# Gate and up projections by Strassen's method with seven quarter products, feed-forward groups four blocks wide

## The chip, the cores and the metric

The kernel runs on one NeuronCore of a Trainium2 chip. The metric is the device time of one execution in microseconds (us). The engines are named as the profile names them: PE (TensorE, with its weight loads as PEld), DVE (VectorE), ACT (ScalarE), POOL (GpSimd) and SP (the queue that issues most transfers). SBUF is the on-chip memory that the engines work from; PSUM is the small memory of eight banks into which PE writes its products.

## The reference

Two layers of an encoder, for 640 tokens (512 of a prompt and 8 x 16 of samples), model width 1024. Each layer has three mixing branches, an output projection, a feed-forward part and a gated projection of a second input. The change touches the feed-forward part alone:

```
x = x + merged @ prm['w_out']
hf = rms_norm(x, prm['norm_ffn'])
g, up = jnp.split(hf @ prm['w_ffn_in'], 2, axis=-1)
x = x + (jax.nn.silu(g) * up) @ prm['w_ffn_out']
ple_gate = jax.nn.sigmoid(rms_norm(x, prm['norm_ple']) @ prm['w_ple_gate'])
```

`w_ffn_in` is 1024 x 5632: 2816 columns of the gate and 2816 of up. `w_ffn_out` is 2816 x 1024. All is float32.

## The kernel before

**Layout.** Activations lie transposed: 128 partitions of features by 640 tokens, eight such slices for the model width. A projection gives 128 output features for two halves of 320 tokens, each half in its own PSUM bank, and runs over eight slices of the contraction (k = 0 to 7).

**Float32 by three products.** Each operand is split into a high part, rounded to PE's fast float format (ACT, a copy), and a low part, the rest (DVE, one subtraction). A product is the sum of three matmuls: high x high, high x low, low x high. So one projection of 128 features takes 8 x 2 x 3 = 48 matmuls of 320 columns (`rows`; the matmuls are recorded at L274).

**Weights.** They come in chunks of 128 x 1024 numbers (512 KB), in the order of a table of units that is made before the kernel (`layer_units`). `load_chunk` issues the transfer into `raw` (two buffers) and records the split into `hi` (ACT, L220) and `lo` (DVE, L221), with a priority ahead of the other work; `hi` and `lo` have three buffers each. `next_chunk` keeps three chunks loaded ahead.

**Feed-forward part.** The 2816 hidden features are 22 blocks of 128, in groups of 8, 8 and 6. For each block (`u_ffn`) the gate chunk and the up chunk give 48 matmuls each. DVE scales the products by the norm of the token (`scaled`, L338) out of PSUM, ACT takes the silu of the gate (L756), POOL multiplies (L760), ACT and DVE split the result into the group's `mid` tiles (L277, L278). After the last block of a group the eight slices of the down projection run over the group's blocks (`u_ffo`): 8 x 2 x 3 = 48 matmuls a slice for a group of 8, and DVE adds them to `x` (L741).

**The norm.** `norm` scales each slice of `x` by the gain (ACT, L307), makes its low part (DVE, L308), squares it (ACT, L309) and sums the squares (DVE, L311). PE adds over the partitions (tile `cs`), POOL takes the power (L317), and PE spreads the result over the partitions (tiles `sp`). The scale of a token is applied to the products, not to the operands, so PE starts on slice k as soon as that slice is split.

**Order.** The program is recorded in the order of the units. A scheduler then sets each engine's order by priority and by its own estimates, and gives each tile a buffer; every engine works through its list in that order, and an instruction that waits holds up all behind it on its engine. Products lie in four PSUM banks (tile `pd`); a bank is free again when DVE (or ACT) has read it.

Of the kernel before, what the change touches and what calls it, by code (L numbers as in the profile page):

```python
# [9 lines left out]
F32 = mybir.dt.float32  # L10
# [11 lines left out]
NT = NP + NS  # L22
# [45 lines left out]
def layer_units():  # L68
    units = []

    def full(name, arg, w, cols):
        units.append((name, arg, [_chunk(w, range(KD), cols)]))

    def av(j):
        c = _cols("av", 256 * j, 256)
        units.append(("av", j, [_chunk("w_in", range(0, 4), c), _chunk("w_in", range(4, 8), c)]))

    def branch(b, c):
        ch = [_chunk("w_in", range(KD), _cols("g" + b, 128 * c, 128))]
# [41 lines left out]
CHUNKS = [ch for u in UNITS for ch in u[2]]  # L121
NCH = len(CHUNKS)
CHW = [sum(len(c) for _, _, c in ch) for ch in CHUNKS]

C_ID, C_CM, C_ADM, C_CMS, C_T, C_BO, C_IND, C_PAR, C_N = 0, 128, 256, 384, 400, 416, 418, 426, 442
G_MIX, G_FFN, G_PLE, G_BIAS, G_Q, G_K, G_N = 0, 8, 16, 24, 48, 49, 50
# [41 lines left out]
        self.kind, self.gen, self.due, self.held, self.past = kind, gen, due, False, False  # L168


class Net:
    def __init__(self, tc, A, cst, big, wp, wk, sm, ps):
        nc = tc.nc
# [30 lines left out]
    def load_chunk(self, pieces=1, also=None):  # L204
        nc, i = self.nc, self.n_loaded
        self.n_loaded += 1
        w = CHW[i % NCH] // pieces
        raw = self.wp.tile([128, 1024], F32, tag="raw", name=f"raw{i}", bufs=2)
        hi = self.wp.tile([128, 1024], F32R, tag="hi", name=f"hi{i}")
        lo = self.wp.tile([128, 1024], F32R, tag="lo", name=f"lo{i}")  # L210
        low = nc.gpsimd if LO_POOL[0] <= i % NCH < LO_POOL[1] else nc.vector
        for p in range(pieces):
            c = slice(w * p, w * p + w)
            nc.sync.dma_start(raw[:, c], self.A["w"][i // NCH, i % NCH, :, c])
            if also:
                also(p)

            def split(c=c):
                with self.tc.high_priority(offset=200):
                    nc.scalar.activation(hi[:, c], raw[:, c], AF.Copy)  # L220
                    low.tensor_tensor(lo[:, c], raw[:, c], hi[:, c].bitcast(F32), op=OP.subtract)  # L221
# [66 lines left out]
    def qk2(self, name):  # L288
        return self.ps.tile([128, 2, 512], F32, tag="qk", name=name, bufs=NQ)

    def pair(self, pool, tags):
        return [pool.tile([128, KD, NT], F32R, tag=t, name=t, bufs=1) for t in tags]

    def norm(self, x, g0, xh, xl):
        nc, gl = self.nc, self.gl
        acc = self.wk.tile([128, NT], F32, tag="t", name="nacc")
        for k in range(KD):
# [18 lines left out]
        nc.vector.tensor_scalar(rsc, cs[:, :5], 1.0 / D, EPS, op0=OP.mult, op1=OP.add)  # L316
        nc.gpsimd.tensor_tensor(rsc, rsc, self.half[:, :5], op=OP.pow)  # L317
# [28 lines left out]
    def layer(self, l):  # L346
# [1 line left out]
        self.S = S = {}  # L348
        self.sc, self.si = [], []
        self.busy = False  # L350
        self.mh = self.norm(self.x, G_MIX, *self.pair(self.big, ("xh", "xl")))
# [372 lines left out]
    def u_out(self, c, ch):  # L724
        S = self.S
        if c == 0:
            mh, ml = self.pair(self.big, ("xh", "xl"))
# [9 lines left out]
    def addx(self, c, pt):  # L737
        x = self.S["x"]
        for h in range(2):
            sl = slice(HN * h, HN * h + HN)  # L740
            self.nc.vector.tensor_tensor(x[:, c, sl], x[:, c, sl], pt[h][:, :HN], op=OP.add)  # L741

    def u_ffn(self, a, ch):
        nc, S = self.nc, self.S
        gi, m = a
        first = gi == 0 and m == 0
        if first:
            S["fx"] = self.norm(S["x"], G_FFN, *self.pair(self.at, ("fh", "fl")))
# [7 lines left out]
        nc.scalar.activation(g, g, AF.Silu)  # L756
# [3 lines left out]
        nc.gpsimd.tensor_tensor(u, u, g, op=OP.mult)  # L760
        self.split(S["mid"][0][:, m], S["mid"][1][:, m], u)

    def u_ffo(self, a, ch):
        gi, c = a
        self.addx(c, self.rows(ch[0], 0, FGROUPS[gi], *self.S["mid"], both=(c == 0)))

    def u_ple(self, c, ch):
        nc, S, l = self.nc, self.S, self.l
        if c == 0:
            S["fx"] = self.norm(S["x"], G_PLE, *self.pair(self.at, ("fh", "fl")))  # L770
            pb = self.at.tile([128, 2, 2, NT], F32R, tag="pb", name="pb", bufs=1)
            for k in range(2):
                pr = self.at.tile([128, NT], F32, tag="lb", name="pr")
# [446 lines left out]
```

## Time and profile before

| | |
|---|---|
| median of 3 runs | 2503.01 us (2500.07 to 2503.66) |
| the profiled execution | 2500.76 us, its span 2499.0 us |
| granted PE clock | 0.995 |
| PE busy, share of the span | 2443.1 us, 98% |
| DVE | 1357.0 us, 54% |
| ACT | 935.5 us, 37% |
| POOL | 317.6 us, 13% |
| feed-forward part, each layer | 466.84 us, of which DVE is busy 197.6 us and ACT 113.5 us |

The profile shows one execution. Busy time counts instructions in work; a matmul's own duration (about 309 ns) overlaps with the next, which starts 147 ns later. The feed-forward part runs from the end of the output projection to the first matmul of the gated projection behind it: from 711.61 to 1178.45 us in the first layer and from 1954.04 to 2420.88 us in the second.

### The profile page before, as it was taken

The numbers are of one execution on the slowest core, as the hardware profiler recorded it, in microseconds if no ns is written. First come the engines' busy times: TensorE is split into PE (matmuls) and PEld (weight loads), VectorE is DVE, ScalarE is ACT, GpSimd is POOL, SyncE is SP. The second block draws the span as 40 slices with busy tenths as digits, with TensorE's granted clock in tenths as the row PEclk, the third lists the DMA queues.
The fourth block names the chain that finished last, engine by engine and source line by source line (L and its number), as shares of the span: only waits on it lengthen the run. The fifth ranks groups of instructions, "written<-read, shape, count | busy, mean of one in ns | idle before, by whom it ended". The sixth has DMA issues, their size and how long they took to land. (4 is left out here: it accounts for less than half of the span.)

```text
span 2499.0 us, 42360 instructions
## 1 busy us (share of the span) xinstructions
PE 2443.1 (98%) x17528; PEld 2335.2 (93%) x17528; DVE 1357.0 (54%) x2447; ACT 935.5 (37%) x1361; POOL 317.6 (13%) x375
## 2 busy tenths in 40 slices
PE   8989999999999999999999999999999999999999
PEld 8887788899999999999999877888999999999999
DVE  5885865544544344345558858556446443443454
ACT  5654466522332122123345454655224221221231
POOL 1122421100001001010011323220000010110100
PEclk9999999999999999999999999999999999999999
DMA  6223244532322222222342232445323222222222
GB/s 200 86 74 88 70 142 138 182 102 74 125 75 76 77 71 74 76 72 81 100 144 87 68 92 87 128 147 166 101 76 129 77 75 77 69 77 76 70 84 75
DMA packets 102399, 242.89 MB, mean 97 GB/s; under 512 B 11152, under 2 KB 33952, under 8 KB 102208
## 3 DMA queue, kind: packets, MB, share of 16 engines
q1 hardware_dynamic: 99552, 229.81, 29.7%
q0 software_dynamic: 2656, 10.38, 1.2%
q8 instruction: 138, 2.26, 0.4%
q14 instruction: 53, 0.43, 0.1%
HBM read 221.07 MB, written 19.08 MB: 96 GB/s over the span
## 5 line engine op out<-in xcount | busy, mean ns | idle before, releaser
L220 ACT ACTIVATE hi<-raw 128x1024 fp32r<-128x1024 f32 (+4 forms) x306 | 316.4, 1035 | 1093.5 <-PE pd L274 654.7
L274 PE MATMUL pd<-fh,lo 128*128 128x320 f32 x1664 | 513.5, 309 | 0.0
L274 PE MATMUL pd<-fh,hi 128*128 128x320 f32 x1664 | 513.4, 309 | 0.0
L274 PE MATMUL pd<-fl,hi 128*128 128x320 f32 x1664 | 513.1, 308 | 0.0
L274 PE MATMUL pd<-xh,hi 128*128 128x320 f32 x1568 | 497.1, 318 | 0.0
L274 PE MATMUL pd<-xh,lo 128*128 128x320 f32 x1568 | 490.9, 313 | 2.4 <-DVE lo L221 2.4
L274 PE MATMUL pd<-xl,hi 128*128 128x320 f32 x1568 | 491.4, 314 | 0.0
L221 DVE TENSOR_TENSOR lo<-raw,hi 128x1024 fp32r<-128x1024 f32 (+4 forms) x268 | 366.7, 1369 | 141.0 <-ACT hi L220 139.9
L274 PEld LDWEIGHTS pd<-fh,hi 128*128 128x128 f32 x1664 | 312.4, 188 | 0.1
L274 PEld LDWEIGHTS pd<-fh,lo 128*128 128x128 f32 x1664 | 312.4, 188 | 0.0
L274 PEld LDWEIGHTS pd<-fl,hi 128*128 128x128 f32 x1664 | 312.4, 188 | 0.0
L274 PEld LDWEIGHTS pd<-xh,hi 128*128 128x128 f32 x1568 | 297.0, 190 | 15.2 <-issue 13.5
L274 PE MATMUL pd<-mid,hi 128*128 128x320 f32 x1408 | 309.9, 308 | 0.0
L274 PEld LDWEIGHTS pd<-xl,hi 128*128 128x128 f32 x1568 | 297.3, 190 | 7.3 <-issue 6.1
L274 PEld LDWEIGHTS pd<-xh,lo 128*128 128x128 f32 x1568 | 297.2, 190 | 7.0 <-DVE lo L221 2.9
L274 PEld LDWEIGHTS pd<-mid,hi 128*128 128x128 f32 x1408 | 235.4, 188 | 0.0
L274 PE MATMUL pd<-mid,lo 128*128 128x320 f32 x704 | 217.0, 308 | 0.0
L760 POOL TENSOR_TENSOR fu<-fu,fg 128x640 f32<-128x640 f32 x44 | 68.9, 1566 | 772.2 <-DVE fu L338 772.2
L741 DVE TENSOR_TENSOR x<-x,pd 128x320 f32<-128x320 f32 x128 | 61.6, 486 | 193.4 <-PE pd L274 192.0
L338 DVE TENSOR_TENSOR fu<-pd,rs 128x320 f32<-128x320 f32 x88 | 43.2, 491 | 192.0 <-PE pd L274 192.0
L274 PEld LDWEIGHTS pd<-mid,lo 128*128 128x128 f32 x704 | 132.2, 188 | 0.0
L338 DVE TENSOR_TENSOR gt<-pd,rs 128x320 f32<-128x320 f32 x96 | 47.0, 490 | 154.8 <-PE pd L274 154.5
(264 smaller groups left out, 3730.5 us busy)
## 6 DMA issues: line engine op xcount, KB each, us to landing
raw<-w SPq DMA_DIRECT2D x270, 512.0 KB, 3.6
kc<-c_k SPq DMA_DIRECT2D x64, 256.0 KB, 4.6
kc<-c_v SPq DMA_DIRECT2D x64, 256.0 KB, 3.5
raw<-w SPq DMA_DIRECT2D x16, 384.0 KB, 3.1
raw<-w SPq DMA_DIRECT2D x11, 468.0 KB, 3.8
ka<-b_k SPq DMA_DIRECT2D x16, 256.0 KB, 3.4
kv<-b_v SPq DMA_DIRECT2D x16, 256.0 KB, 3.3
x<-xT SPq DMA_DIRECT2D x8, 320.0 KB, 6.0
```

What stands on the lines that cost most here:

```text
L220: nc.scalar.activation(hi[:, c], raw[:, c], AF.Copy)
L221: low.tensor_tensor(lo[:, c], raw[:, c], hi[:, c].bitcast(F32), op=OP.subtract)
L274: self.nc.tensor.matmul(out, a, b, start=start, stop=stop)
L338: self.nc.vector.tensor_tensor(dst[:, sl], pt[h][:, :HN], self.rs[:, sl], op=OP.mult)
L741: self.nc.vector.tensor_tensor(x[:, c, sl], x[:, c, sl], pt[h][:, :HN], op=OP.add)
L760: nc.gpsimd.tensor_tensor(u, u, g, op=OP.mult)
```

## The change

**Seven products in place of eight.** For one block take the gate rows and the up rows of the weights, each in two halves of the contraction (k = 0 to 3 and 4 to 7): A11, A12 (gate) and A21, A22 (up); and the normed activations in the same halves and in two halves of the tokens: B11, B12 and B21, B22. The two outputs for two halves of tokens are eight products of such quarters before. Now they are seven: A11 B11, A12 B21, S1 T1, S2 T2, S3 T3, S4 B22 and A22 T4, with S1 = A21 + A22, S3 = A11 - A21, S2 = A22 - S3, S4 = A12 - S2, and T1 = B12 - B11, T3 = B22 - B12, T2 = B11 + T3, T4 = B21 - T2. Each has 4 slices x 3 matmuls = 12 matmuls of 320 columns, in one PSUM bank, so a block takes 84 matmuls where it took 96. The outputs are sums of the products: `u2` = A11 B11 + S2 T2, `u3` = `u2` + S3 T3, `u4` = `u2` + S1 T1; gate = (A11 B11 + A12 B21, `u4` + S4 B22), up = (`u3` + A22 T4, `u3` + S1 T1).

**The weights' sums** are made on the chip, for every block, from the two raw chunks (`load_second`): four sums of 128 x 512 on DVE, and five splits of 128 x 512 (ACT the high part, DVE the low), for S1, S3, S2, A22 and S4. The first chunk of a block is split as before. The second raw chunk has one buffer of its own (`rawb`), S2 to S4 have four (`sh`, `sl`).

**The activations' sums** are made once a layer (`norm_quarters`): for k = 0 to 3 the scaled slice, its split for B11, T1 and its split; for k = 4 to 7 T3, T2, T4 and B21, B22 with their splits. B11, T1, T2, T3 lie in `fh` and `fl`, and B21, B22, T4 in `xh` and `xl`, which the output projection reads up to its end.

**The products' sums** replace `scaled`: ACT copies A11 B11 out, DVE makes seven sums of 128 x 320 out of PSUM, then multiplies up and gate by the norm, 128 x 640 each. Silu, product and split follow as before.

**Groups and order.** The 22 blocks are in groups of 4, 4, 4, 4, 3 and 3, with two buffers for `mid`. The eight slices of a group's down projection are dealt out among the blocks of the next group, and one chunk holds two slices; those of the last group follow at the end. A slice of a group of four takes 24 matmuls. The sums into `x` (two a slice, on DVE) are now for 6 x 8 slices in place of 3 x 8. The second input's transfers (`pr`) and split (`pb`), which stood at the beginning of the output projection, use the buffers of `mid` and stand in the last group's down projection.

```diff
-FGROUPS = (8, 8, 6)
+FGROUPS = (4, 4, 4, 4, 3, 3)
...
+            if gi:
+                for c in range(KD * m // n, KD * (m + 1) // n):
+                    ffo(gi - 1, c)
+    for c in range(KD):
+        ffo(gi, c)
...
+    def load_second(self, i):
+
+        nc, r0 = self.nc, self.raw
+        r1 = self.at.tile([128, 1024], F32, tag="rawb", name=f"raw{i}", bufs=1)
+        nc.sync.dma_start(r1, self.A["w"][i // NCH, i % NCH])
...
+        def split(src, h, l):
+            nc.scalar.activation(h, src, AF.Copy)
+            nc.vector.tensor_tensor(l, src, h.bitcast(F32), op=OP.subtract)
...
+            nc.vector.tensor_tensor(s1, r1[:, a], r1[:, b], op=OP.add)
+            split(s1, hi[:, a], lo[:, a])
...
+            nc.vector.tensor_tensor(s3, r0[:, a], r1[:, a], op=OP.subtract)
+            own(s3)
...
+            nc.vector.tensor_tensor(s2, r1[:, b], s3, op=OP.subtract)
+            own(s2)
+            split(r1[:, b], hi[:, b], lo[:, b])
...
+            nc.vector.tensor_tensor(s4, r0[:, b], s2, op=OP.subtract)
+            own(s4)
...
+    def norm_quarters(self, x, g0):
...
+            nc.scalar.activation(q, xk, AF.Copy, scale=g)
...
+            nc.scalar.activation(sq, x[:, k], AF.Square)
+            if k < 4:
+                self.split(o1[0][:, 0, j], o1[1][:, 0, j], q[:, 0])
+                nc.vector.tensor_tensor(b[:, j, 0], q[:, 1], q[:, 0], op=OP.subtract)
+                self.split(o1[0][:, 1, j], o1[1][:, 1, j], b[:, j, 0])
+            else:
+                p = a[:, j]
+                nc.vector.tensor_tensor(p[:, 1], q[:, 1], p[:, 1], op=OP.subtract)
+                nc.vector.tensor_tensor(p[:, 0], p[:, 0], p[:, 1], op=OP.add)
+                self.split(o1[0][:, 2:4, j], o1[1][:, 2:4, j], p)
+                self.split(o2[0][:, 0:2, j], o2[1][:, 0:2, j], q)
+                nc.vector.tensor_tensor(q[:, 0], q[:, 0], p[:, 0], op=OP.subtract)
+                self.split(o2[0][:, 2, j], o2[1][:, 2, j], q[:, 0])
...
-        pg = self.rows(ch[0], 0, KD, *S["fx"], both=first)
...
-        self.scaled(pg, g)
...
+        p1 = prod("A11", "B11")
+        nc.scalar.activation(r1, p1, AF.Copy)
+        if first:
+            p5, p7 = prod("S1", "T1"), prod("S3", "T3")
+        p6 = prod("S2", "T2")
...
+        add(u2, p6, r1)
+        if not first:
+            p7 = prod("S3", "T3")
+        add(u3, p7, u2)
+        if not first:
+            p5 = prod("S1", "T1")
+        add(u[:, t], p5, u3)
+        add(u4, p5, u2)
+        add(g[:, h], prod("A12", "B21"), r1)
+        add(u[:, h], prod("A22", "T4"), u3)
+        nc.vector.tensor_tensor(u, u, rs, op=OP.mult)
+        add(g[:, t], prod("S4", "B22"), u4)
+        nc.vector.tensor_tensor(g, g, rs, op=OP.mult)
         nc.scalar.activation(g, g, AF.Silu)
```

In the built program PE has 15,880 matmuls and transposes where it had 16,408; DVE has 3,043 instructions where it had 2,319, ACT 1,523 where it had 1,263, POOL and SP as many as before. Up to the output projection of a layer every engine's order is what it was. Line numbers in the rows below are those of the changed kernel where they stand for it (L242 is the old L221, L335 the old L278, L806 the old L741; L262, L272 to L282 are the weights' sums and their low parts, L872 the products' sums, L897 and L899 the products with the norm).

**DVE, a block inside the second group.** Before, from the scaling of one block's gate on to the next (`fg` the gate, `fu` up, `lo` a chunk's low part, `mid1` the low part of the result):

```order
L338 TENSOR_TENSOR fg_8246<-pd_8196,rs_7504 128x320
L338 TENSOR_TENSOR fg_8246<-pd_8197,rs_7504 128x320
L221 TENSOR_TENSOR lo89_8192<-raw89_8190,hi89_8191 128x1024
L338 TENSOR_TENSOR fu_8300<-pd_8250,rs_7504 128x320
L338 TENSOR_TENSOR fu_8300<-pd_8251,rs_7504 128x320
L221 TENSOR_TENSOR lo90_8308<-raw90_8306,hi90_8307 128x1024
L278 TENSOR_TENSOR mid1_7453<-fu_8300,mid0_7452 128x640
```

After, the part of a block between its S2 T2 and the multiplication of up by the norm (`xh2` holds r1, u2, u3, u4, `xl2` the gate, `sl` the low parts of S2 to S4):

```order
L872 TENSOR_TENSOR xh2_7552<-pd_8727,xh2_7552 128x320
L262 TENSOR_TENSOR sl_8835<-s2_8832,sh_8834 128x512
L872 TENSOR_TENSOR xh2_7552<-pd_8741,xh2_7552 128x320
L872 TENSOR_TENSOR fu_8712<-pd_8755,xh2_7552 128x320
L872 TENSOR_TENSOR xh2_7552<-pd_8755,xh2_7552 128x320
L872 TENSOR_TENSOR xl2_7553<-pd_8770,xh2_7552 128x320
L242 TENSOR_TENSOR lo94_8708<-raw94_8706,hi94_8707 128x1024
L872 TENSOR_TENSOR fu_8712<-pd_8784,xh2_7552 128x320
L262 TENSOR_TENSOR lo95_8821<-s1_8822,hi95_8820 128x512
L262 TENSOR_TENSOR lo95_8821<-raw95_8818,hi95_8820 128x512
L282 TENSOR_TENSOR s4_8840<-raw94_8706,s2_8832 128x512
L897 TENSOR_TENSOR fu_8712<-fu_8712,rs_7610 128x640
```

The sums that free the banks stand between the weights' splits and sums of the block that comes next.

**ACT and DVE, the beginning of the feed-forward part.** ACT after, around the last slice (k = 7) of the activations (`qb` and `qa` the scaled slices and their sums, `xh` the high parts of B21, B22, T4, `fh` those of T2, T3, `xh2` the copy of A11 B11, chunk 77 the second one of block 1):

```order
L824 ACTIVATE qb_7453<-x_6927,gcol0_74 128x640
L826 ACTIVATE nsq_7531<-x_6927 128x640
L334 ACTIVATE xh_7489<-qb_7453 128x2x320
L880 ACTIVATE xh2_7552<-pd_7557 128x320
L334 ACTIVATE xh_7489<-qb_7453 128x320 x3
L261 ACTIVATE hi77_7424<-s1_7426 128x512
L261 ACTIVATE hi77_7424<-raw77_7422 128x512
L334 ACTIVATE fh_7450<-qa_7452 128x2x320
L261 ACTIVATE sh_7438<-s2_7436 128x512
```

DVE after, a little later (chunks 78 and 79 are those of block 2; pd_7597 is S2 T2 of block 0, pd_7584 S3 T3, pd_7571 S1 T1):

```order
L262 TENSOR_TENSOR sl_7447<-s4_7444,sh_7446 128x512
L275 TENSOR_TENSOR s3_7686<-raw78_7672,raw79_7678 128x512
L272 TENSOR_TENSOR s1_7682<-raw79_7678 128x512
L278 TENSOR_TENSOR s2_7692<-raw79_7678,s3_7686 128x512
L335 TENSOR_TENSOR xl_7490<-qb_7453,xh_7489 128x320
L872 TENSOR_TENSOR xh2_7552<-pd_7597,xh2_7552 128x320
L872 TENSOR_TENSOR xh2_7552<-pd_7584,xh2_7552 128x320
L872 TENSOR_TENSOR fu_7556<-pd_7571,xh2_7552 128x320
L242 TENSOR_TENSOR lo78_7674<-raw78_7672,hi78_7673 128x1024
L872 TENSOR_TENSOR xh2_7552<-pd_7571,xh2_7552 128x320
```

Where one split for each slice stood, the weights' splits of the next blocks now stand ahead of the last slice's split on ACT, and ahead of the sums that empty the banks on DVE.

More of the change, by code (lines that the diff above doesn't have):

```diff
@@ L168, in __init__, with __getitem__ @@
         self.kind, self.gen, self.due, self.held, self.past = kind, gen, due, False, False
+class Parts:
+    def __init__(self, tiles):
+        self.tiles = tiles
+    def __getitem__(self, at):
+        p, k, *rest = at
+        return self.tiles[k // 6][(p, k % 6, *rest)]
 class Net:
@@ L207, in load_chunk @@
         w = CHW[i % NCH] // pieces
+        if i % NCH in SECOND:
+            return self.load_second(i)
         raw = self.wp.tile([128, 1024], F32, tag="raw", name=f"raw{i}", bufs=2)
+        self.raw = raw
         hi = self.wp.tile([128, 1024], F32R, tag="hi", name=f"hi{i}")
@@ L289, in qk2, with pair_big @@
         return self.ps.tile([128, 2, 512], F32, tag="qk", name=name, bufs=NQ)
+    def pair_big(self):
+        return [Parts([self.big.tile([128, n, NT], F32R, tag=t + i, name=t + i, bufs=1) for n, i in ((6, ""), (2, "2"))])
+                for t in ("xh", "xl")]
     def pair(self, pool, tags):
@@ L350, in layer @@
         self.busy = False
-        self.mh = self.norm(self.x, G_MIX, *self.pair(self.big, ("xh", "xl")))
+        self.mh = self.norm(self.x, G_MIX, *self.pair_big())
         if l:
@@ L726, in u_out @@
         if c == 0:
-            mh, ml = self.pair(self.big, ("xh", "xl"))
+            mh, ml = self.pair_big()
             for k in range(KD):
@@ L747, in u_ffn @@
         if first:
-            S["fx"] = self.norm(S["x"], G_FFN, *self.pair(self.at, ("fh", "fl")))
+            S["fq"], S["sp"] = self.norm_quarters(S["x"], G_FFN)
+            S["mids"] = {}
         if m == 0:
-            S["mid"] = self.pair(self.at, ("mid0", "mid1"))
-        pg = self.rows(ch[0], 0, KD, *S["fx"], both=first)
+            S["mids"][gi] = [self.at.tile([128, 4, NT], F32R, tag=t, name=t) for t in ("mid0", "mid1")]
+        mid, ops, sp = S["mids"][gi], S["fq"], S["sp"]
+        (h0, l0), (h1, l1, own) = ch
@@ new lines, in u_ffn, with prod @@
+        W = {"A11": (h0, l0, 0), "A12": (h0, l0, 512), "S1": (h1, l1, 0), "A22": (h1, l1, 512)}
+        W.update({n: (h, l, 0) for n, (h, l) in zip(("S3", "S2", "S4"), own)})
+        def prod(w, t):
+            bank = self.ps.tile([128, 512], F32, tag="d", name="pd", bufs=ND)[:, :HN]
+            wh, wl, o = W[w]
+            xh, xl = ops[t]
+            for k in range(4):
+                ws = slice(o + 128 * k, o + 128 * k + 128)
+                for i, (p, q) in enumerate(((wh, xh), (wh, xl), (wl, xh))):
+                    self.mm(bank, p[:, ws], q[:, k], start=(k == 0 and i == 0), stop=(k == 3 and i == 2))
+            return bank
@@ new lines, in add @@
+        def add(out, x, y):
+            nc.vector.tensor_tensor(out, x, y, op=OP.add)
+        r1, u2, u3, u4 = (sp[0][:, HN * i:HN * i + HN] for i in range(4))
+        par = S["par"] = 1 - S.get("par", 1)
+        g = sp[1][:, NT * par:NT * par + NT]
+        u = self.wk.tile([128, NT], F32, tag="t2", name="fu", bufs=1)
+        h, t = slice(0, HN), slice(HN, NT)
+        p1 = prod("A11", "B11")
+        nc.scalar.activation(r1, p1, AF.Copy)
+        if first:
+            p5, p7 = prod("S1", "T1"), prod("S3", "T3")
@@ L756, in u_ffn @@
+        nc.vector.tensor_tensor(u, u, rs, op=OP.mult)
+        add(g[:, t], prod("S4", "B22"), u4)
+        nc.vector.tensor_tensor(g, g, rs, op=OP.mult)
         nc.scalar.activation(g, g, AF.Silu)
-        pu = self.rows(ch[1], 0, KD, *S["fx"])
-        u = self.wk.tile([128, NT], F32, tag="t2", name="fu", bufs=1)
-        self.scaled(pu, u)
         nc.gpsimd.tensor_tensor(u, u, g, op=OP.mult)
-        self.split(S["mid"][0][:, m], S["mid"][1][:, m], u)
+        self.split(mid[0][:, m], mid[1][:, m], u)
@@ L763, in u_ffo @@
     def u_ffo(self, a, ch):
         gi, c = a
-        self.addx(c, self.rows(ch[0], 0, FGROUPS[gi], *self.S["mid"], both=(c == 0)))
+        if c % 2 == 0:
+            self.S["foch"] = ch[0]
+        n = FGROUPS[gi]
+        self.addx(c, self.rows(self.S["foch"], n * (c % 2), n, *self.S["mids"][gi], both=(c == 0)))
     def u_ple(self, c, ch):
```

59 lines of the change are left out of this document (50 added, 9 removed).

## The prediction

> **What bounds the kernel now.** I read the busy shares first, then the clock, then the two feed-forward stretches.
>
> ```profile
> PE 2443.1 (98%) x17528; PEld 2335.2 (93%) x17528; DVE 1357.0 (54%) x2447; ACT 935.5 (37%) x1361; POOL 317.6 (13%) x375
> ...
> PEclk9999999999999999999999999999999999999999
> ```
>
> PE is busy nearly all the time at full clock. The windows of the part that changes, first and second layer:
>
> ```profile
> core 0: us, PE busy (x) PEld busy (x) DVE busy (x) ACT busy (x) POOL busy (x), PEclk, DMA share, GB/s
> 711.61:1178.45 466.84, 466.84 (x3189) 466.60 (x3188) 197.55 (x242) 113.52 (x131) 35.67 (x23) 1.00 0.25 75
> 1954.04:2420.88 466.84, 466.84 (x3189) 466.60 (x3188) 197.57 (x242) 113.51 (x131) 35.66 (x23) 1.00 0.24 75
> ```
>
> PE never stands still in them; DVE is at 42%. The timeline of PE at their beginning shows what is not a 320-column matmul:
>
> ```profile
> 711.61 0.31 PE L274 MATMUL pd<-fh,hi 128*128 128x320 f32 x1
> ...
> 715.57 1.28 PE L274 MATMUL cs<-ones,nacc 128*128 128x1 f32 x10
> 716.71 0.40 PE L274 MATMUL pd<-fh,lo 128*128 128x320 f32 x1
> ...
> 720.02 1.28 PE L274 MATMUL sp<-con,rsc 128*128 128x128 f32 x10
> 721.05 0.40 PE L274 MATMUL pd<-fh,hi 128*128 128x320 f32 x1
> ```
>
> The norm's small matmuls take 716.71 - 715.57 = 1.14 and 721.05 - 720.02 = 1.03 us. The rest is 22 blocks x 96 + 22 x 48 = 3168 matmuls, so one takes (466.84 - 2.17) / 3168 = 0.1467 us. PE's count of matmuls is the time here.
>
> **Removed: 12 matmuls a block.** 12 x 22 x 2 layers = 528, x 0.1467 = 77.4 us. The shape and the order high-high, high-low, low-high stay, so I keep the rate. A block now takes 84 x 0.1467 = 12.3 us on PE, and 19.4 with two slices of a down projection (48 matmuls) between.
>
> **Added to DVE.** The price of one instruction is the step to the next in an unbroken row. Timeline of DVE, a block and a half, then four rows of the norm:
>
> ```profile
> 799.78 2.31 DVE L221 TENSOR_TENSOR lo<-raw,hi 128x1024 fp32r<-128x1024 f32 x1 [0.51 <-ACT hi L220]
> 802.01 0.81 DVE L278 TENSOR_TENSOR mid<-fu,mid 128x640 fp32r<-128x640 f32 x1
> 802.75 0.48 DVE L338 TENSOR_TENSOR fg<-pd,rs 128x320 f32<-128x320 f32 x1
> ...
> 806.82 1.23 DVE L221 TENSOR_TENSOR lo<-raw,hi 128x1024 fp32r<-128x1024 f32 x1 [0.51 <-ACT hi L220]
> ...
> 712.76 1.22 DVE L221 TENSOR_TENSOR lo<-raw,hi 128x1024 fp32r<-128x1024 f32 x1 [0.46 <-ACT hi L220]
> 713.90 0.88 DVE L308 SCALAR_TENSOR_TENSOR fl<-x,gcol,fh 128x640 fp32r<-128x640 f32 x1
> ...
> 722.31 0.88 DVE L338 TENSOR_TENSOR fg<-pd,rs 128x320 f32<-128x320 f32 x2
> ```
>
> 1024 columns: 1.14; 640: 0.74; 320 out of PSUM: 0.40 (two in 0.88, one 0.48). No row has 512 columns; bounds are 0.74 and 0.40, and the line through 1024 and 640 gives 0.60, which I take (0.41 for 320 in SBUF). A block of a group of four then costs: two full chunks 2.28; four sums and five low parts of 512 columns 5.4; seven sums out of PSUM 2.8; two products with the norm 1.48; the result's low part 0.74; four sums into x 1.6. That is 14.3. POOL adds to it:
>
> ```profile
> 799.44 1.57 POOL L760 TENSOR_TENSOR fu<-fu,fg 128x640 f32<-128x640 f32 x1 [12.51 <-DVE fu L338]
> ```
>
> The 1024-column low part that ran into this took 2.31 in place of 1.23: 1.1 us more, in sum 15.4 against PE's 19.4. ACT has less: its 1024, 640 and 512 columns step at about 0.96, 0.64 and 0.53, in sum 6.5 us a block. So in 18 of 22 blocks DVE has 4.0 us to spare, and every bank that it empties is asked for again two to four products (3.5 us and more) later. I cost the added DVE work there at nothing; its cover is the dealt-out down projection. Without that cover, in the first four blocks, DVE has 15.4 - 1.14 - 1.6 = 12.7 against 12.3.
>
> **The beginning of the stretch** is the term against the change. Before, PE needs only slice 7's split. Now S3 T3 and S2 T2 need slice 7's sums and all others, and the tiles of B21, B22, T4 are only free when the output projection ends. Rows used:
>
> ```profile
> 720.07 1.06 ACT L220 ACTIVATE hi<-raw 128x1024 fp32r<-128x1024 f32 x1 [6.00 <-PE pd L274]
> 721.11 0.60 ACT L325 ACTIVATE rs<-sp 128x512 f32<-128x512 f32 x1
> 721.61 0.27 ACT L326 ACTIVATE rs<-sp 128x128 f32<-128x128 f32 x1
> 721.89 1.28 ACT L756 ACT_TABLE_LOAD   x1
> 723.22 0.74 ACT L756 ACTIVATE fg<-fg 128x640 f32<-128x640 f32 x1
> ...
> 815.12 0.74 ACT L277 ACTIVATE mid<-fu 128x640 fp32r<-128x640 f32 x1 [1.30 <-POOL fu L760]
> ```
>
> ```profile
> 717.13 1.21 POOL L317 TENSOR_TENSOR rsc<-rsc,half 128x5 f32<-128x5 f32 x1 [49.98 <-DVE rsc L316]
> ```
>
> I walk the queues from the last matmul of the output projection (0). PE does A11 B11, S1 T1 and slices 4 to 6 of S3 T3, S2 T2, A12 B21 by 7.5. DVE meanwhile ends x (1.6), a chunk's low part (2.7), four low parts of 640 columns and six instructions of 320, so B21's slice 7 stands at 8.1: PE ends A12 B21 at 8.6 (0.6 lost). The squares are summed at 9.6, `cs` runs to 10.9 (1.1 lost). ACT's two halves of chunk 77 wait for A12 B21, and slice 7 of T2, T3 stands behind them: high part 10.6, and low part 12.1 behind three DVE instructions of chunk 77; the last of S3 T3 and S2 T2 end at 12.8 (1.1 lost). The power on POOL ends at 14.0, `sp` at 15.1 (1.2 lost). T4's slice 7 stands on DVE behind two low parts and the three sums of chunk 79 (17.0): A22 T4 ends at 17.4 (0.6 lost). S4 B22 then waits shortly for u2 to empty its bank and ends at 19.4, where 84 matmuls and 2.2 us of norm would end at 14.5: 4.9 lost. In blocks 1 to 3 DVE stops for the result's low part, since silu, POOL and the high part follow one another (0.7 + 1.6 + 0.7) with too little between: 2.9 us in block 1, where the 1.28 us table load stands in this chain, 1.8 in the next two. So u2 of blocks 1 to 4 comes at 23.6, 39.5, 53.0 and 66.6, and PE, slowed by banks that are not empty, ends block 4's last product at 71.2 in place of 63.8. With 0.6 behind it I get 8.0 us a layer, 16 in all. Bounds: nothing (the waits lie beside work), and double (every wait a second time, 16 a layer).
>
> [...]
>
> **The end of the stretch.** The last group's slices take 18 matmuls, 2.6 us, in place of 36, and DVE has about 2.9 a slice (two sums 0.8, norm 1.5, half a chunk 0.6); it ends some 3 us late, while PE has 7 us of gate matmuls on the slices that are ready. The second input arrives in its place twice:
>
> ```profile
> raw<-w SPq DMA_DIRECT2D x270, 512.0 KB, 3.6
> ...
> pr<-pT POOLq DMA_DIRECT2D x4, 320.0 KB, 3.9
> ```
>
> ACT and DVE stand for it, at most 4 us behind the first slice; two slices (5.3) cover that. Without the cover it is 2 x 4 us. I take 0.5 a layer. Chunks land in 3.6 us against 3.5 to 12 between their buffers' release and use. The rest of the program keeps its order.
>
> **Sum.** The profiled execution is 2500.76 us, 2.25 below the median shown. 2500.8 - 77.4 + 16.0 + 1.0 = 2440.4, and 2442.6 against the median: I say 2441.
>
> **Rivals.** *The beginning costs nothing*: 2500.8 - 77.4 + 1 = 2424. For it: today's stretch begins without a gap. Against it: the new chains, 4.9 us of them ahead of any bank. 0.08.
> *It costs double*: 2456. For it: in the first group DVE has more work than PE whatever the order. Against it: 12.7 is only 0.4 more. 0.08.
> *DVE becomes the bound everywhere*, the slower side. Mechanism: DVE works in order and stands at each low part until ACT has its high part.
>
> ```profile
> DVE lo L221 <- ACT hi L220: 139.9, 215, 6.6
> ```
>
> That is 0.65 each on average, 0.51 in the rows above. Eight low parts a block (two full, five half, the result) would give 4.1, the chain ahead of the result's another 2.8: 15.4 + 6.9 = 22.3 against 19.4, so 2.9 x 18 blocks, and 19.6 - 12.3 = 7.3 x 4 in the first group, 81 a layer: 2424 + 162 = 2586. It decides from 4.0 us of waits a block. Against it: in DVE's order sums out of PSUM stand between most high parts and their low parts. 0.05 in full; with half of the excess the time is 2424 + 81 = 2505, as before: 0.02.
> *The waits slow PE's clock*. At the program's start PE stood for 6.8 us:
>
> ```profile
> 8.46 0.46 PE L274 MATMUL pn<-hi,xl 128*128 128x312 f32 x1
> 8.72 0.46 PE L274 MATMUL pn<-hi,xh 128*128 128x312 f32 x1
> ...
> 10.42 0.31 PE L274 MATMUL pn<-lo,xh 128*128 128x312 f32 x1
> 10.56 0.31 PE L274 MATMUL pn<-hi,xh 128*128 128x312 f32 x1
> ```
>
> Its matmuls came every 0.26 us until about 10, then every 0.145. From 6.85 on that is 3.2 x (1 - 0.145 / 0.26) = 1.4 us a time; three times a layer, 2449. No wait in my walk is longer than 2.3 us. 0.05. [...]
>
> **How the numbers follow.** Forecast 0.72, rivals as given (0.08, 0.08, 0.05 and 0.02, 0.05). The forecast's own range is 2431 to 2452 (3.5 to 14 us a layer at the beginning). The range of all but the slower case is 2424 to 2456; no wait in the end stretch or on a DMA is priced there, so I reach to 2465 above, and leave the bare 2424 just outside. A difference within 0.2% (5 us) can't be told from none. Faster 0.93, same 0.02, slower 0.05.
>
> **What would show it.** Each feed-forward stretch at 436 us in place of 467, with 2924 matmuls at 0.147; DVE near 340 us of it; PE's gaps nearly all within 75 us of the stretch's beginning, behind DVE and ACT. PE gaps in the later groups, or low parts that wait for high parts there, would prove the third rival; gaps at the gated projection would prove my 0.5 wrong; spacings of 0.26 the fourth.

## The result, and the profile after

The changed kernel takes 2447.24 us (median of 4 runs, 2446.89 to 2449.37), the kernel before 2503.26 on the same chip: a ratio of 0.9781, 95% interval 0.9764 to 0.9798. The profiled execution took 2446.89 us, its span is 2445.1.

Forecast were 2441 us, and 2440.4 for the profiled execution. So the direction and nearly all of the size held, and 6.5 us of cost are missing from the sum. The busy line of the page:

```profile
PE 2377.1 (97%) x17000; PEld 2263.4 (93%) x17000; DVE 1697.4 (69%) x3171; ACT 1060.5 (43%) x1621; POOL 319.0 (13%) x375
```

528 matmuls fewer, and DVE at 69% in place of 54%. Next the two feed-forward stretches of the changed kernel, each from the first matmul of its first block to the first of the gated projection (columns as in the windows of before):

```profile
712.91:1153.26 440.35, 433.88 (x2927) 431.07 (x2925) 358.01 (x580) 169.23 (x248) 37.52 (x25) 0.99 0.25 80
1927.68:2367.56 439.88, 433.87 (x2926) 430.80 (x2925) 355.36 (x579) 169.27 (x248) 37.47 (x25) 0.99 0.25 80
```

Between the same two matmuls the kernel before has 467.13 and 467.12 us (the windows shown of before are two matmuls shorter). The stretches together give 934.25 - 880.23 = 54.0 us; the rest of the span is 1564.8 before and 1564.9 now. All of the gain is in the stretches. Without the removed matmuls a stretch would be 467.1 - 38.7 = 428.4, so 11.95 and 11.5 us are lost in them, 23.4 in all, where the prediction had 17.

Where they are lost is seen from the starts of the blocks in PE's timeline. Blocks 0 to 5 take 20.83, 12.33, 12.33, 13.76, 22.99 and 19.62 us, where 84 matmuls are 12.32, the two slices of 24 in blocks 4 and 5 make it 19.36, and block 0 has 2.17 for the norm. Blocks 6 to 16 take 19.36 each (block 9 from 872.85 to 892.21); those behind them have more matmuls or fewer, as their groups have three blocks. So 6.3 us go in block 0, 5.3 in blocks 3 to 5, and 0.6 at 1093. That is 0.3 more than 11.95, since the norm is counted at 2.17 us here, while 467.13 less 3168 matmuls leaves some 2.5 for it. PE's timeline in block 0, with its gaps in brackets:

```profile
720.39 0.31 PE L331 MATMUL pd<-xh,hi 128*128 128x320 f32 x1
721.94 0.41 PE L331 MATMUL pd<-xl,hi 128*128 128x320 f32 x1 [1.24 <-DVE xl L335]
...
723.48 2.24 PE L331 MATMUL cs<-ones,nacc 128*128 128x1 f32 x10 [0.98 <-DVE nacc L840]
725.58 0.88 PE L331 MATMUL pd<-fh,sh 128*128 128x320 f32 x2
726.26 0.47 PE L331 MATMUL pd<-fl,sh 128*128 128x320 f32 x1
726.53 0.47 PE L331 MATMUL pd<-fh,sl 128*128 128x320 f32 x1
...
727.79 2.50 PE L331 MATMUL sp<-con,rsc 128*128 128x128 f32 x10 [0.26 <-POOL rsc L383]
729.94 0.60 PE L331 MATMUL pd<-xh,hi 128*128 128x320 f32 x1
```

The waits are those of the walk: A12 B21 for B21's slice 7 (`xl`), `cs` for the sum of squares, `sp` for POOL. But from `cs` on everything is slow: `cs` takes 725.58 - 723.48 = 2.10 us and `sp` 2.15, where they took 1.14 and 1.03, and matmuls step by 0.27. The windows of PE alone in this place (us, PE busy, granted clock, DMA) say why:

```profile
720.00:721.00 1.00, 0.69 (x5) 1.00 0.00 0
721.00:722.00 1.00, 0.06 (x1) 1.00 0.00 0
722.00:723.00 1.00, 0.49 (x2) 1.00 0.00 0
723.00:724.00 1.00, 0.52 (x3) 0.78 0.00 0
724.00:725.00 1.00, 1.00 (x7) 0.50 0.00 0
...
730.00:731.00 1.00, 1.00 (x8) 0.80 0.00 0
```

The clock was halved. If a mean of 0.78 is full clock and then half, it fell at 723.56, and it rose at 730.40: 6.84 us.

The waits behind block 0, from the same timeline, and DVE's, from its own:

```profile
776.34 0.38 PE L331 MATMUL pd<-fh,sh 128*128 128x320 f32 x1 [2.25 <-DVE xh L872]
...
789.61 0.42 PE L331 MATMUL pd<-mid,hi 128*128 128x320 f32 x1 [0.86 <-DVE xh L872]
...
1093.32 0.41 PE L331 MATMUL pd<-fh,sh 128*128 128x320 f32 x1 [0.30 <-DVE x L806]
```

```profile
742.51 0.83 DVE L335 TENSOR_TENSOR mid<-fu,mid 128x640 fp32r<-128x640 f32 x1 [2.80 <-ACT mid L334]
756.53 0.83 DVE L335 TENSOR_TENSOR mid<-fu,mid 128x640 fp32r<-128x640 f32 x1 [1.71 <-ACT mid L334]
770.62 0.83 DVE L335 TENSOR_TENSOR mid<-fu,mid 128x640 fp32r<-128x640 f32 x1 [1.55 <-ACT mid L334]
784.59 0.83 DVE L335 TENSOR_TENSOR mid<-fu,mid 128x640 fp32r<-128x640 f32 x1 [1.70 <-ACT mid L334]
```

PE's longest wait is at S2 T2 of block 4, for a bank that a sum of DVE empties. DVE stands at the low part of each block's result, 2.8 us in block 1 and 1.6 to 1.7 after, with sums queued behind it.

### The profile page after: what moved, and what is told of

It reads as the page before. It is cut to its first block, busy times and chain, and to the rows that moved or that the text cites. A ratio compares the mean times of both kernels' runs of the same rounds, so it can differ in the third digit from the quotient of the medians.

```text
span 2445.1 us, 42376 instructions
## 1 busy us (share of the span) xinstructions
PE 2377.1 (97%) x17000; PEld 2263.4 (93%) x17000; DVE 1697.4 (69%) x3171; ACT 1060.5 (43%) x1621; POOL 319.0 (13%) x375
## 5 line engine op out<-in xcount | busy, mean ns | idle before, releaser
L331 PE MATMUL pd<-xh,hi 128*128 128x320 f32 x1920 | 607.7, 317 | 0.5 <-DVE xh L872 0.5
L331 PE MATMUL pd<-xl,hi 128*128 128x320 f32 x1920 | 600.3, 313 | 2.3 <-DVE xl L335 2.3
L331 PE MATMUL pd<-xh,lo 128*128 128x320 f32 x1920 | 599.9, 312 | 2.4 <-DVE lo L242 2.4
L242 DVE TENSOR_TENSOR lo<-raw,hi 128x1024 fp32r<-128x1024 f32 (+4 forms) x224 | 264.6, 1182 | 80.4 <-ACT hi L241 79.3
L331 PE MATMUL pd<-fh,hi 128*128 128x320 f32 x608 | 187.9, 309 | 0.1
L331 PE MATMUL pd<-fl,hi 128*128 128x320 f32 x608 | 187.5, 308 | 0.0
L331 PE MATMUL pd<-fh,lo 128*128 128x320 f32 x608 | 187.4, 308 | 0.0
L331 PE MATMUL pn<-hi,xh 128*128 128x312 f32 (+1 forms) x400 | 120.1, 303 | 9.4 <-ACT xh L368 7.0
L806 DVE TENSOR_TENSOR x<-x,pd 128x320 f32<-128x320 f32 x224 | 105.9, 481 | 23.2 <-PE pd L331 21.5
L331 PE MATMUL pn<-hi,xl 128*128 128x312 f32 (+1 forms) x400 | 119.4, 300 | 0.0
L331 PE MATMUL pn<-lo,xh 128*128 128x312 f32 (+1 forms) x400 | 119.0, 299 | 0.0
```

The costliest lines, as they stand in the source:

```text
L331: self.nc.tensor.matmul(out, a, b, start=start, stop=stop)
```

## The experiments

The table has every kernel that was run. The stretch is measured as above; "rest" is the span less the two stretches. The rest differs by up to 7 us between kernels. The part ahead of the first stretch differs although PE's order there is the same: the stretch starts at 712.91 in the changed kernel, at 716.17 in late_split and at 710.47 in late_six0. So the stretches, and not the times alone, carry the comparisons of a few microseconds.

| kernel | median us | ratio to before, 95% interval | stretches us | rest us |
|---|---|---|---|---|
| the change | 2447.24 | 0.9781 (0.9764 to 0.9798) | 440.35, 439.88 | 1564.9 |
| groups_only | 2504.11 | 1.0008 (0.9999 to 1.0017) | 467.12, 467.13 | 1568.4 |
| no_deal | 2491.65 | 0.9957 (0.9942 to 0.9972) | 458.33, 459.47 | 1570.3 |
| keep_clock | 2446.79 | 0.9778 (0.9765 to 0.9792) | 438.89, 439.70 | 1566.8 |
| six_banks | 2456.96 | 0.9818 (0.9805 to 0.9832) | 445.27, 443.59 | 1567.7 |
| two_first | 2450.20 | 0.9793 (0.978 to 0.9806) | 442.28, 441.52 | 1566.4 |
| two_first_fill | 2454.78 | 0.9806 (0.9793 to 0.982) | 442.05, 443.47 | 1568.8 |
| two_first_five | 2455.16 | 0.9817 (0.9803 to 0.9831) | 442.21, 447.36 | 1563.8 |
| dve_plus | 2583.4, one run | | | |
| late_split | 2437.75 | 0.9741 (0.9728 to 0.9755) | 434.73, 435.86 | 1568.0 |
| late_split_fill | 2441.54 | 0.9754 (0.9741 to 0.9767) | 435.77, 436.62 | 1567.8 |
| late_six0 | 2441.30 | 0.9755 (0.9742 to 0.9769) | 437.14, 437.62 | 1563.2 |
| late_split_fill14 | 2443.26 | 0.9758 (0.9744 to 0.9771) | 437.07, 436.91 | 1568.6 |

**groups_only: Strassen undone, groups and dealing out kept.**

```diff
-SECOND = {int(_at[i]) + 1 for i, u in enumerate(UNITS) if u[0] == "ffn"}
+SECOND = set()
...
+        pg = self.rows(ch[0], 0, KD, *S["fx"], both=first)
...
+        pu = self.rows(ch[1], 0, KD, *S["fx"])
...
```

> The groups of four blocks and the dealt-out down projection stay; the gate and up projections are the eight plain quarter products of before (96 matmuls a block). If the gain is the count of matmuls alone, the feed-forward stretch is 466.8 us again, PE without a wait in it, and the time 2503 us (2498 to 2508). If the dealing out itself gains or costs something (other waits, other chunks), the time differs from 2503 by more than 5 us and PE shows gaps or the stretch is shorter.

The windows of its first stretch:

```profile
716.07:1183.19 467.12, 467.12 (x3190) 466.87 (x3189) 215.58 (x288) 115.39 (x133) 36.83 (x25) 1.00 0.25 76
```

As expected: the stretch of before to a hundredth, PE busy throughout, and 2504.11 us. Dealing the down projection out is worth nothing by itself. The gain is the count of matmuls.

**no_deal: seven products, each group's down projection behind its group.**

```diff
-            if gi:
-                for c in range(KD * m // n, KD * (m + 1) // n):
-                    ffo(gi - 1, c)
-    for c in range(KD):
-        ffo(gi, c)
+        for c in range(KD):
+            ffo(gi, c)
```

> The seven products stay, but each group's down projection comes behind its own group instead of between the blocks of the next. The theory of the prediction (the down projection's 7.1 us of PE a block is what DVE's work hides behind): DVE has 12.8 us a block against PE's 12.3 in all 22 blocks, the waits that the first group now shows come in every group (3 to 5 us), and each group's end stands 2 to 3 us for the last block's result: 30 to 40 us a layer, 2447 + 60 to 80, about 2515 us, no faster than before. The rival (banks and buffers are enough in any order, DVE is not near a bound): within 10 us of 2447.

PE's waits in its first stretch, and the windows of the stretch:

```profile
PE pd L328 <- ACT mid L331: 13.5, 6, 2.9
...
PE pd L328 <- DVE xl L869: 0.9, 2, 0.6
```

```profile
715.48:1173.81 458.33, 441.30 (x2926) 436.98 (x2925) 347.03 (x580) 168.60 (x247) 37.37 (x25) 0.98 0.24 77
```

The loss is 18 to 20 us a layer and not 30 to 40, and 2491.65 us lies between the 2515 of the theory and the rival's 2457. PE idles 17.0 us a stretch against 6.5, 13.5 of it at the six group ends, where the last block's result is not there yet; and PE's busy time grows by 7.4 us (441.30 - 433.88) at a mean clock of 0.98, since the clock is halved behind some of these waits (behind one of 2.90 us, matmuls step by 0.27 us from 1154.89 on). The third part of the expectation fell: waits for banks inside the blocks hardly appear. Behind block 0, the blocks that another block of their group follows take 12.32 us, their 84 matmuls alone, but for one of 12.65 (first layer). So a down projection behind four blocks lets DVE catch up as well as one dealt out between them; what the dealing out hides is the wait for a group's last result. So Strassen without dealing out gains 10 us, and with it 56: this is the part of the change that looked like bookkeeping.

**keep_clock: 18 matmuls in block 0's waits.**

```diff
...
+                    nc.tensor.matmul(spare[:, 0, :HN], h0[:, 0:128], ops["B11"][0][:, 0], start=True, stop=True)
...
-        add(g[:, h], prod("A12", "B21"), r1)
+        p2 = prod("A12", "B21")
+        fill(18)
+        add(g[:, h], p2, r1)
```

> 18 matmuls more in the first block of each layer, into a bank that nobody reads, on operands that are ready, placed where PE stands in block 0: 5 in the wait for slice 7 of A12 B21 (1.24 us), 9 ahead of cs (wait 0.98 us) and 4 ahead of slice 7 of S3 T3. They take 2.6 us of PE at full clock, 1.6 of them in waits. Theory 1 (the half clock from 723.6 to 730.4 is set by PE's idleness just before, and it is what makes block 0 cost 2.5 us more than walked): the clock stays 1.00, cs takes 1.14 and sp 1.03 us, block 0 ends 1.5 to 2.5 us sooner a layer, and the time is 2442 to 2445. Theory 2 (the slow matmuls come from operands that arrive late or from a transfer at the same time): cs still takes about 2.1 and sp 2.15 us, spacings of 0.26 stay, and the time is 2447 to 2450.

PE's timeline in blocks 0 and 1:

```profile
724.06 1.17 PE L331 MATMUL cs<-ones,nacc 128*128 128x1 f32 x10
...
726.78 1.38 PE L331 MATMUL sp<-con,rsc 128*128 128x128 f32 x10
...
734.24 0.41 PE L331 MATMUL pd<-fh,sh 128*128 128x320 f32 x1 [0.58 <-ACT xh L887]
```

The granted clock is 1.00 in every microsecond from 719 to 733, `cs` takes 1.03 us and `sp` 1.14, and block 0 takes 18.38 in place of 20.83 us although it has 18 matmuls more. So PE's idleness ahead of `cs` made the slow microseconds, and it costs 2.45 us in block 0, net of what the filling takes. That part of theory 1 held; its time did not. The stretches are only 1.5 and 0.2 us shorter and the time is 2446.79, since blocks 1 to 4 now have a wait of 0.58 or 0.59 us each that the changed kernel has not, and two of 1.2 and 1.5 us follow in blocks 4 and 5, where the changed kernel has 2.25 and 0.86: blocks 1 to 5 take 6.9 us more than their matmuls, where it was 5.3. The four stand at S2 T2 and end with ACT's copy of A11 B11 out of its bank, so there the two products have one and the same bank; in the changed kernel no S2 T2 of a first-group block waits for that copy. The scheduler, with other work to place, had dealt the banks anew.

**six_banks: two products a block in the banks that stand idle.**

```diff
+            if t in ("B21", "T4"):
+                bank = two[:, int(t == "T4"), :HN]
+            else:
+                bank = self.ps.tile([128, 512], F32, tag="d", name="pd", bufs=ND)[:, :HN]
```

> A12 B21 and A22 T4 of every block go to the two banks that the feed-forward part leaves idle, so the products have six banks and not four; nothing else changes. Theory 1 (PE's waits behind DVE's sums in blocks 1 to 5 are waits for an emptied bank): the waits of 0.2 to 2.3 us at 758 to 799 go (5.3 us a layer), and in block 0 the twelve matmuls of S4 B22 stand in the wait for slice 7, 1.8 us a layer and perhaps the half clock with it: 2447 - 2 x 7 = 2433, at best 2428. Theory 2 (DVE's work in the first group is the limit, 12.8 us a block against 12.3, and more banks only move the wait to the next place): 2443 to 2447, with waits as long at another bank.

PE's waits in its first stretch, those that the changed kernel has not:

```profile
PE pd L331 <- DVE xl L877: 3.9, 5, 1.2
```

It lost 4 to 5 us a layer, and 2456.96 us is outside both theories. The two banks are one tile, and a matmul into one half waits until DVE has read the other: A22 T4 stands for the sum of A12 B21, up to 1.2 us, in later groups too, where nothing waited before, and a block of the later groups takes 19.48 us in place of 19.36. Block 0 takes 20.99 us: `cs` came at full clock (1.26 us), but behind a wait of 1.48 us for slice 7 the clock was halved all the same (`sp` takes 2.16 us). This run measured the shared tile; it says little about banks.

**two_first, two_first_fill, two_first_five: the first group cut to two blocks.**

```diff
-FGROUPS = (4, 4, 4, 4, 3, 3)
+FGROUPS = (2, 4, 4, 4, 4, 4)
```

> Groups of 2, 4, 4, 4, 4, 4 blocks in place of 4, 4, 4, 4, 3, 3: the same products, sums and chunks, but only two blocks have no down projection beside them, and the second group has two slices of 24 matmuls a block (15.8 us of PE against some 15 of DVE). Theory 1 (PE's waits at 758 to 799 are DVE's lag of four blocks without cover): these 5.3 us a layer shrink to 1 or 2, 2447 - 2 x 4 = 2439, and block 0 with its half clock stays. Theory 2 (the lag is made in block 0, by the chains behind slice 7, and must be paid whatever follows): the waits stay in sum, only at other places, 2445 to 2449.

> The same groups, with the 18 filling matmuls of keep_clock in block 0 of each layer. Keep_clock alone won 2.0 us in block 0 (clock 1.00, cs 1.03, sp 1.14) and lost them again at banks in blocks 1 to 5 (8.2 us of gaps in place of 5.3). If it was lost because DVE, not PE, sets the pace of the first four blocks, then here, where DVE has cover from block 2 on, most of it stays won: 3 to 4 us below two_first. If the loss has another cause (the bank that the fills take, the changed order), it is lost here too: two_first within 1 us.

> The same groups, and A22 T4 of every block goes to one of the two idle banks, so the products have five banks with nothing shared. Six_banks, where two products shared a tile of two banks, was 10 us slower: PE then stood for the second product's sum (up to 1.2 us, some 6 us a layer outside the first group) and 0.1 us in every block. If that sharing was its loss, five single banks lose nothing: two_first or up to 3 us below it. If the change of banks itself is the loss (other order on PE and DVE), it is 3 to 10 us above two_first.

The windows of two blocks of the second group in two_first, which have two slices of 12 matmuls each, 108 matmuls or 15.84 us:

```profile
783.05:800.12 17.07, 16.64 (x111) 15.86 (x110) 15.53 (x26) 6.33 (x10) 1.57 (x1) 1.00 0.23 74
800.12:817.18 17.06, 16.63 (x110) 15.84 (x110) 15.39 (x26) 6.33 (x10) 1.57 (x1) 1.00 0.29 94
```

The loss of blocks 3 to 5 came back in another form, and larger: these blocks take 17.06 us, 1.2 more than PE's work, and blocks 2 to 6 together 8 us more. Theory 1 fell. Theory 2 is nearer, though 2450.20 us lies just above its 2445 to 2449, and that the lag is made in block 0, as it says, is not shown by this run. DVE's work in these blocks, 15.4 to 15.5 us, is less than PE's 15.84; but DVE gets through it only in 17. In the other two kernels the expectations missed or say little: with the filling (2454.78, 4.6 us above two_first, where the same time or 3 to 4 us less was expected) block 0 is 18.3 us again and later waits take it back, S2 T2 for ACT's copy among them. A fifth bank (2455.16, in the range of the case that the change of banks is the loss) brings neither gain nor loss in the first layer (442.21) and 5.8 us of loss in the second. There PE's clock is halved from 1942.02 for 6.83 us, where in the first layer it is from 726.88 for 3.41, and once more from 1986.39 for 3.41, when a wait for a sum into x has lasted 2.64 us (1.15 at the same place in the first layer). So most of that loss is clock, and the run tells little of banks.

**dve_plus: extra work for DVE.**

```diff
+EXTRA = (0, 4, 8, 12, 16, 20)
...
+                nc.vector.tensor_tensor(dz[:, :HN], u4 if i else u2, r1, op=OP.add)
```

> More work for DVE: 4, 8, 12, 16 and 20 sums of 320 columns in each block of groups 1 to 5, into a bank that nobody reads, 0.40 us each: 1.6, 3.2, 4.8, 6.4 and 8.0 us a block. PE has 19.4 us a block there (21.7 in group 4, with its 64 matmuls of down projection). Theory 1 (DVE has 4.0 us to spare a block, its waits cost nothing): groups 1 and 2 at 19.4 a block, group 3 about 0.9 over, group 4 about 0.7 and group 5 about 4 over: some 18 us a layer, 2482 in all. Theory 2 (DVE's waits for high parts and banks eat its slack, it is at its bound already): every added microsecond shows but the first, 50 to 60 us a layer, 2550 to 2565. Theory 3 (more to spare than counted): under 2460.

Windows of one block of group 1 (1.6 us added), of group 2 (3.2) and of group 3 (4.8):

```profile
822.70:842.06 19.36, 19.36 (x134) 19.36 (x133) 17.39 (x31) 6.87 (x11) 1.57 (x1) 1.00 0.26 83
880.80:901.30 20.50, 19.76 (x135) 19.40 (x134) 18.94 (x35) 6.80 (x11) 1.83 (x1) 1.00 0.23 78
948.80:976.80 28.00, 22.22 (x135) 21.99 (x134) 21.36 (x38) 6.97 (x10) 1.88 (x1) 0.88 0.19 65
```

In these blocks 1.6 us cost nothing, 3.2 cost 1.1, and 4.8 cost 8.6. So DVE had between 1.6 and 3.2 us to spare, some 2.1 if the cost rises one for one (an estimate from these three), and not 4.0. The time, 2583.4, is above all three theories. Blocks 4 and 5, just behind the first group, do pay for the 1.6 (26.61 and 23.03 us in place of 22.99 and 19.62), and the cost does not rise evenly: 6.4 us in the three blocks of group 4 cost 2.2, 3.3 and 6.7. Beyond the spare time the two engines wait for each other: at 968.81 PE waits 5.78 us for sums into x that stand in DVE's row behind low parts, and then DVE waits for PE; the clock falls as well, to a mean of 0.88 in the third window. A count of work does not show this.

**late_split: the result's split behind the next block's fourth sum.**

```diff
-        nc.gpsimd.tensor_tensor(u, u, g, op=OP.mult)
-        self.split(mid[0][:, m], mid[1][:, m], u)
+        nc.gpsimd.tensor_tensor(g, u, g, op=OP.mult)
+        S["due"] = (mid[0][:, m], mid[1][:, m], g)
...
         add(u4, p5, u2)
+        self.late()
...
```

> Only the place of the result's split changes: its high part on ACT and its low part on DVE are issued behind the fourth sum of the next block (and the product with silu goes to the gate's buffer, so that the up half's buffer comes free as before). In the changed kernel DVE stands at this low part for 2.80, 1.71, 1.55 and 1.70 us in blocks 1 to 4, 7.8 us a layer, with sums queued behind it. Theory 1 (DVE's standing there is what empties PE's banks too late at 758 to 799): DVE takes the sums first, the 5.3 us of waits fall to 1 or 2, 2447 - 2 x 4 = 2439. Theory 2 (DVE's work alone is too much for the first blocks, its waits lie beside it): the waits stay, 2445 to 2449.

Its stretches, and all of PE's waits in the first:

```profile
716.17:1150.90 434.73, 432.38 (x2927) 431.07 (x2925) 356.49 (x580) 169.27 (x248) 37.31 (x25) 0.99 0.25 80
1925.05:2360.91 435.86, 432.28 (x2926) 430.83 (x2925) 357.01 (x580) 169.32 (x248) 37.50 (x25) 0.99 0.25 80
```

```profile
PE pd L331 <- DVE xl L335: 1.2, 1, 1.2
PE cs L331 <- DVE nacc L840: 1.0, 1, 1.0
PE sp L331 <- POOL rsc L383: 0.2, 1, 0.2
```

The largest of DVE's waits from the stretch's beginning to 800, first in the changed kernel, then in this one:

```profile
DVE mid L335 <- ACT mid L334: 7.8, 4, 2.8
```

```profile
DVE fu L872 <- POOL xl L902: 2.9, 2, 2.0
```

Theory 1: the stretches are 5.6 and 4.0 us shorter, and the time is 2437.75 where 2439 was expected. Blocks 1 to 4 take 12.32, 12.32, 12.32 and 19.78 us; of the waits those of block 0 are left. DVE's work in the stretch is the same (356.5 and 358.0 us); it now stands for POOL's product, 2.9 us and not 7.8. So the waits in blocks 3 to 5 were not DVE's amount of work but its standing at the result. This kernel beats both.

**late_split_fill, late_six0, late_split_fill14: block 0 again, on top of that.** The first has keep_clock's 18 matmuls. In late_six0 A22 T4 and S4 B22 of block 0 go to the idle banks (`if first and t in ("T4", "B22")`), so that useful matmuls fill the waits. The third has 14 filling matmuls, a number with which S2 T2 keeps a bank of its own.

> The later split together with the 18 filling matmuls of keep_clock. If DVE's standing at the result's low part is what took keep_clock's 2.0 us of block 0 back, it stays won here: 3 to 5 us below late_split, 2435. If DVE's work alone sets the pace of blocks 0 to 4, it is within 1 us of late_split.

> The later split; and in the first block of each layer A22 T4 and S4 B22 go to the two banks that the feed-forward part leaves idle, so that nine matmuls of A22 T4, which wait for no slice 7, stand in PE's waits of block 0: useful work in the place of keep_clock's filling. If PE's idleness there is the cost: the clock stays 1.00, block 0 ends 3 to 4 us sooner than in late_split, 2432. If DVE sets the pace: within 2 us of late_split, and the waits come back in blocks 1 to 5.

> The later split with 14 filling matmuls in block 0 (5 and 9, not the last 4). In keep_clock and late_split_fill the scheduler had given S2 T2 of block 1 (and of 2 to 4, by the waits) the bank that A11 B11 of the same block had just filled, so PE stood for ACT's copy of it, 0.6 us and 0.1 behind it a block; with 14 the two have different banks in the first six blocks, as in late_split. If that allotment took the gain of the full clock back, the stretch to the gated norm's cs is 440.7 - 2.3 = 438.4 us in the first layer, without waits on ACT's copy, and the time about 2433 (the part ahead of the stretch alone differs by up to 3 us a layer between these kernels). If DVE sets the pace of the first blocks whatever PE does, the stretch stays at 440 to 441 and the time at 2438.

All three miss. One wait of PE from each of the first two (their first stretches), and from late_split_fill14 PE's at `sp` with DVE's row ahead of it:

```profile
PE pd L331 <- ACT xh L887: 1.8, 3, 0.6
```

```profile
PE pd L331 <- ACT xh L885: 1.2, 2, 0.6
```

```profile
731.15 2.50 PE L331 MATMUL sp<-con,rsc 128*128 128x128 f32 x10 [3.38 <-POOL rsc L383]
```

```profile
728.65 0.68 DVE L282 TENSOR_TENSOR s<-raw,s 128x512 f32<-128x512 f32 x1
729.25 0.48 DVE L335 TENSOR_TENSOR xl<-qb,xh 128x320 fp32r<-128x320 f32 x1
729.65 0.16 DVE L382 TENSOR_SCALAR rsc<-cs 128x5 f32<-128x5 f32 x1
```

The first gains 2.3 us in block 0 (18.36 against 20.71) and loses 3.4 behind it, most of it to the one bank that A11 B11 and S2 T2 share again. The second puts nine matmuls of A22 T4 into the waits, but its clock is halved all the same at 723.6 (`sp` takes 2.15 us): blocks 0 and 1, across whose border S4 B22 has moved, take 33.0 us together as in late_split, and waits for ACT's copy come on top. In the third no wait is left behind block 0, but there the scheduler put four of the next chunk's instructions ahead of the norm's 5 columns on DVE: `cs` ends at 726.65, DVE comes to it at 729.65, `sp` waits 3.38 us, the clock is halved in that wait, from 729.66 on (`sp` takes 2.50), and block 0 takes 23.1. Whether the 2.3 us of block 0 can be kept, with both orders held as in late_split, was not run and stays open.

## Why the prediction was right, and where it was short

*The matmuls removed* (77.4 us): shown. Undone alone they give the old stretch, and a block of the later groups takes 19.36 us against 19.4.

*DVE's prices*: right. The 512-column instructions step by 0.60 us and the sums out of PSUM by 0.40, and in blocks 6 to 16 (814.77 to 1027.73) DVE is busy for 173.78 of 212.96 us, 15.8 a block against 15.4. (357 us a stretch and not 340: the norms' own instructions at both ends were left out of that count.) *DVE's 4.0 us to spare*: wrong by half. It was the difference of two sums of work; dve_plus and two_first put it near 2.2. At the change's own load it costs nothing, as forecast: from 791 to the end PE idles 0.3 us.

*The beginning* (8.0 a layer) is the term that was mis-sized: 11.6 in the first layer. Most of its waits are where the walk has them: B21's slice 7 (0.6 forecast, 1.24 measured), `cs` (1.1 and 0.98), `sp` (1.2 and 0.26), then one long wait and one of 0.6 behind it (2.25 at S2 T2 of block 4, and 0.86), and DVE's stops at the result (2.9, 1.8 and 1.8 forecast; 2.8, 1.7 and 1.55 measured). Two are not seen as waits: slice 7 of S3 T3 and S2 T2 (1.1), and of A22 T4 (0.6); there PE was slow instead. The sizes were off in both directions. Block 0 lost 6.3 and not 4.9, and the runs say why: the half clock, worth 2.45 there, was put at nothing. Without it (keep_clock) block 0 loses 3.9, so the walk's waits alone came out 1 us too dear and hid part of the clock's cost. Blocks 3 to 5 lost 5.3, where the walk had 3.1: the two long waits make 3.4, four small ones of 0.16 to 0.43 another 1.2, and the matmul behind a wait steps by some 0.25 in place of 0.15 us, 0.65 in sum. That all of this hangs on DVE's stops is shown by late_split, where it is gone.

*The end of the stretch* (0.5 a layer): near in size, by luck. ACT does wait for the second input's transfer, 2.73 us at 1135.82, and DVE behind it 1.12, but PE has no wait there. What is lost is 0.6 us at 1093, in the first layer alone, where a bank waits for a sum into x.

*The rivals.* Three of the four did not come. The clock's came in part: the sign that the prediction gives for it, spacings of 0.26 us, is there in block 0 (0.27 from 726.26 to 727.06), and its time, 2449, is nearer to 2447.24 than the 2441 that was forecast. That it is so near is luck, as it counts three slow spells a layer of 1.4 us each, and there was one, worth 2.45; what else is missing from the sum lies in blocks 3 to 5. It was set aside with the words that no wait is longer than 2.3 us. That is the reasoning that failed: two waits of 1.24 and 0.98 us with little between halved the clock, for 6.84 us.

## What to carry to other kernels

When work is moved from TensorE to VectorE, count what VectorE does in order and where it must stand, not only its sum: here its sum of work was 4 us a block under PE's, and it had some 2 to spare. The instruction that waits longest in a row (a result behind a chain over three engines) belongs behind the ones that free banks; moving it was worth 9.6 of the 23.4 us that the change loses in the two stretches. A small change in one place can let the scheduler deal banks and order anew in another, so compare stretches and single waits, not only the time.

## What had not been expected of the hardware

In the changed kernel the clock fell behind short waits that came together, 1.24 and 0.98 us, and stayed at half while PE was at work again. PE was busy 0.69, 0.06 and 0.49 of the three microseconds ahead of the fall, and 5.74 of the six from 724 to 730, all of them at 0.50; half clock lasted 6.84 us. In no_deal it fell 1.3 us after the end of a single wait of 2.44 us (858.70 to 861.14). Its windows of PE alone:

```profile
861.00:862.00 1.00, 0.86 (x6) 1.00 0.00 0
862.00:863.00 1.00, 1.00 (x7) 0.74 0.00 0
863.00:864.00 1.00, 1.00 (x6) 0.50 0.00 0
...
865.00:866.00 1.00, 1.00 (x5) 0.55 0.00 0
866.00:867.00 1.00, 1.00 (x9) 1.00 0.00 0
```

By the same reading it lasted from 862.48 to 865.90, 3.42 us: half of 6.84. In the same kernel a wait of 2.37 us at 1022 left the clock at 1.00, and so did the 2.25 us at 774 in the changed one. So the length of a single wait does not tell these cases apart.

Two stretches of each kernel, as long as the shorter spell of half clock: one that ends with a fall, and one that begins inside the long wait that left the clock at 1.00 (first the changed kernel, then no_deal):

```profile
720.14:723.56 3.42, 1.19 (x7) 1.00 0.00 0
774.76:778.17 3.41, 1.83 (x13) 1.00 0.97 360
```

```profile
859.07:862.48 3.41, 1.34 (x9) 1.00 0.13 52
1022.91:1026.33 3.42, 1.84 (x12) 1.00 0.05 17
```

PE is busy for 1.19 and 1.34 us of the stretches behind which the clock falls. But in the changed kernel it was busy for only 0.74 us of the three from 774 to 777, less than the 1.24 of the three from 720 to 723, and the clock stayed at 1.00. And in six_banks the clock fell behind 3.41 us (724.33 to 727.74) with 1.93 us busy, in which most of the norm's ten one-column matmuls lie. What decides whether a wait brings the clock down, and for how long, is not shown by these runs.
